# A transformer trunk in float32 on one core: four groups of seven products behind the last 256 columns, with a planner that counts work

## The chip, the cores and the metric

The kernel runs on one core of a Trainium2 chip. Its time is the device time of one execution in microseconds (us). A core has TensorE (PE in the profile, PEld is its weight load), VectorE (DVE), ScalarE (ACT), GpSimd (POOL) and SyncE (SP), each with an instruction queue of its own that it works off in order, and 16 DMA engines.

## What is computed

Two layers on 256 tokens of width 1024, all in float32, then a last RMSNorm. The change concerns the four channel mixers (two SwiGLUs in each layer, 2816 wide):

```python
def swiglu(h, w_gate, w_up, w_down):
    return (jax.nn.silu(h @ w_gate) * (h @ w_up)) @ w_down

for l in range(DEPTH):                     # DEPTH = 2, D_MODEL = 1024, SEQ = 256, D_FF = 2816
    x = x + 0.5 * swiglu(rms_norm(x, ffn1_norm[l]), ffn1_w_gate[l], ffn1_w_up[l], ffn1_w_down[l])
    ...                                    # two kinds of attention, x = x + concat(out_a, out_b) @ w_out[l]
    x = x + 0.5 * swiglu(rms_norm(x, ffn2_norm[l]), ffn2_w_gate[l], ffn2_w_up[l], ffn2_w_down[l])
return rms_norm(x, final_norm)
```

In the order of execution there are four of them, called FFN1 to FFN4 here; a mixer with attention stands between FFN1 and FFN2 and between FFN3 and FFN4.

## The kernel before

**Splits.** Every float32 operand is held as a high part (a cast to fp32r) and a low part (the remainder), and every product is three matmuls: high by high, low by high, high by low. For weights, ACT makes the high part (`CAST w<-raw`) and DVE the low part (`w<-raw,w`), in halves of 128x1024. A *split* is one such half. Weights come by DMA of SP into six tiles `raw`, 1 MB each; split halves lie in a pool of 28 tiles of 128 partitions x 1024 that they share with h and x.

**The FFN.** The 2816 columns are five groups of 512 and a rest of 256. Of each group, gate and up are computed (8 weight steps of 128 rows in `tokens`, for two blocks of 128 tokens), then `gate` (silu on ACT), `hidden` (the product with up, on DVE: `s<-ps,hr,tmp`), then `turn`: eight transposes of h on PE, a cast on ACT and a subtraction on DVE per half. The transposed h goes into the down matmuls (`down`), whose four accumulators `accs` stay open in PSUM over the whole FFN. The down matmuls of group g-1 are done inside group g, in two halves of the output columns, each with a weight step of its own.

**Seven products.** For groups 2, 3 and 4 (`SEVEN`) the gate and up product is seen as a 2x2 block product, two blocks of tokens by two halves of the contraction on one side and gate and up on the other, and done with seven block products in place of eight (`by_seven`). One block product (`prod`) is 12 matmuls of 128x512. It needs sums of blocks: of x (`make_sums`, four sums, each with a subtraction or addition on DVE, a cast on ACT and a subtraction on DVE, into tiles `q` and `v`), of weights, and of the products. The tiles of weights of a group are a and d (gate, first and second half of the contraction) and b and c (up). Sums of weights are made in place: c is added to b and b to a by *gathers*, which are DMAs of POOL that read the weights again and add them to the tile, and two more (c to a, d to a) by DVE (`raw<-raw,raw`). The products p2 to p7 are combined by DVE (`put`, `tmp<-ps,tmp`); g0 and g1 go through the silu, and `up` makes the two halves of h.

**The order of the work.** PE, ACT, DVE and POOL keep the order of the program (`Kept`), except in parts of the attention. The order of weight steps is a list `specs`; `ahead(n)` emits splits up to half n, sums of weights (`prep`) and DMAs as far ahead as tiles are free. `weights()` takes the next step and calls `ahead` with a look of `look[0]` halves, set by hand (8 in an FFN, 6 in the mixer). So the place of a split in DVE's and ACT's queues is fixed by the calls of `weights()`. After the groups, FFN and mixer are joined by `ffn_close`, which finishes the down matmuls (`group` for those of group 4, `tail` for those of the rest), adds them to the residual xk (`res.add`) and starts the next norm (`pair`, `squares`, `stats`; `stats` ends with a power on POOL that gives r). At the very end `close` and `finish` do so for the output.

**Order of an FFN before:** group 0 plain, group 1 plain (with the sums of x), groups 2 to 4 as seven products, the last 256 columns (`gu`), then the end. In FFN1 the constants of the attention are made at the end of `ffn` (`aside`).

Of the kernel before, what the change touches and what calls it, by code (L numbers as in the profile page):

```python
# [27 lines left out]
AHEAD = 10  # L28
N_RAW, N_S4 = 6, 28
IN_FFN, IN_MIX = 8, 6  # L30
SEVEN = (2, 3, 4)
# [3 lines left out]
def trunk(ctx: ExitStack, tc: tile.TileContext, x, n1, g1, u1, d1, nm, w_in, sink,  # L35
# [111 lines left out]
    def emit_dma(i):  # L147
        s = specs[i]
        raws[s.key] = raw = wp.tile([P, s.kn, s.n], F32, tag="raw", bufs=N_RAW, name=nm_("raw"))
        for dst, src in s.moves(raw):  # L150
            if i > 1:
                sp.dma_start(dst, src)
            else:
                for k in range(s.kn):
                    sp.dma_start(dst[:, k:k + 1], src[:, k:k + 1])
                    yield
        if s.behind is not None:
            s.behind()
# [52 lines left out]

    def ahead(n):

        n = min(n, 2 * len(specs) - 1)
        while True:
            if at["split"] <= n and at["prep"] > at["split"] // 2:
                for _ in emit_split(*divmod(at["split"], 2)):
                    pass
                at["split"] += 1
            elif at["prep"] <= min(n // 2 + 1, len(specs) - 1) and at["dma"] > at["prep"] and \  # L220
                    (specs[at["prep"]].prep is None or at["split"] >= 2 * at["prep"]):
                if specs[at["prep"]].prep is not None:
                    specs[at["prep"]].prep()
                at["prep"] += 1
            elif at["dma"] < min(at["use"] + AHEAD, len(specs)) and (specs[at["dma"]].moves is None or len(raws) < N_RAW):
                if specs[at["dma"]].moves is not None:
                    for _ in emit_dma(at["dma"]):
                        pass
                at["dma"] += 1
            else:  # L230
                break
# [11 lines left out]
    for l in range(DEPTH):  # L243
        def ffn_specs(wg, wu, wd):
            down = lambda g, h: plain(wd[l], h * 512, 512, 4 * g, 4)
            for k0 in (0, 4):
                specs.extend(plain(w[l], 0, 512, k0, 4) for w in (wg, wu))
            for g in range(1, NGRP):
                downs = [down(g - 1, h) for h in range(2)]
                if g in SEVEN:  # L250
                    specs.extend(seven(wg[l], wu[l], g * 512, downs))
                else:
                    specs.extend(plain(w[l], g * 512, 512, k0, 4) for w in (wg, wu) for k0 in (0, 4))
                    specs.extend(downs)
            for k0 in (0, 4):
                def gu_moves(t, k0=k0, ws=(wg[l], wu[l])):
                    return [(t[:, :, h * 256:h * 256 + 256], rows(w, FF - 256, 256, k0, 4)) for h, w in enumerate(ws)]
                specs.append(Step(4, 512, gu_moves))
            specs.append(down(NGRP - 1, 0))
            specs.append(plain(wd[l], 0, D, 4 * NGRP, 2))  # L260
            specs.append(down(NGRP - 1, 1))
# [17 lines left out]
        for k0 in (0, 2):  # L279
# [3 lines left out]
            specs.append(Step(2, D, o_moves))  # L283
        fine.update(range(mixed + 2, len(specs)))
# [5 lines left out]
    class Norm:  # L290


        def __init__(self, g0, sums=len(SEVEN) > 0):
            self.g0, self.xs, self.sums = g0, [], sums
            self.xg, self.turned = [], []
            self.ss = tmp("nss", 2, (P, 2, 4))
# [36 lines left out]
        def make_sums(self):  # L333
# [5 lines left out]
            def make(x, y, op):  # L339
# [4 lines left out]
                act.copy(sm[:, :, 0:P], v)  # L344
                dve.tensor_tensor(sm[:, :, P:S], v, f(sm[:, :, 0:P]), op=ALU.subtract)
# [3 lines left out]
            s1 = make(b1, t1, ALU.subtract)  # L349
            yield  # L350
            s2 = make(s1, t0, ALU.add)
            yield
            make(t1, t0, ALU.subtract)
            yield
            make(b0, s2, ALU.subtract)
# [12 lines left out]
        def stats(self, n=512):  # L368
# [7 lines left out]
            dve.tensor_scalar_mul(self.hr, self.r, 0.5)  # L376

# [189 lines left out]
    def ffn(norm, aside=None, before=None, final=False):  # L567
# [31 lines left out]
        def by_seven(h, g):  # L599

# [6 lines left out]

            m1, m7 = flat(), flat()
            act.copy(m1, prod(norm.quarter(0, 0), weights()))
            act.copy(m7, prod(norm.summed(2), weights(held=True)))  # L610
            hT = turn(h, 2)
            p2 = prod(norm.quarter(0, 1), weights())
            g0 = put(flat(), p2, m1, ALU.add)
            p3 = prod(norm.summed(3), weights())
            silu(g0, g0, 0)
            down(hT, g - 1, 0, weights())
            h = blk(F32)
            p5 = prod(norm.summed(0), weights())
            late = g == max(SEVEN)
            p6 = prod(norm.summed(1), weights(look[0] - 5 if late else 0, late))  # L620
            u2 = put(flat(), p6, m1, ALU.subtract)
            u3 = put(m7, m7, u2, ALU.add)
            p4 = prod(norm.quarter(1, 1), weights(look[0] - 4 if late else 0, late))
            g1 = put(m1, p4, u3, ALU.subtract)
            w = weights(look[0] - 3 if late else 0)
            silu(g1, g1, 1)
            put(u3, u3, p5, ALU.subtract)
            put(u2, u2, p5, ALU.subtract)
            put(u2, u2, p3, ALU.add)
            up(h, u2, g0, 0)  # L630
            up(h, u3, g1, 1)
            down(hT, g - 1, 1, w)
            return h

        def turn(hs, n):
            out_ = []
            for i in range(n):
# [11 lines left out]
        def down(hT, g, h, w):  # L649
            tokens(accs[h], [None] * (2 * g) + hT, w, 4 * g, last=(FC - 1, G4 - 1) if final and h else FC - 1)  # L650
# [14 lines left out]
        tokens(gs, norm.xs, weights(), 4)  # L665
        g = gate(gs)
        tokens(us, norm.xs, weights(), 4)
        h = hidden(g, us)
        for n in range(1, NGRP):
            sums = norm.make_sums() if n + 1 == min(SEVEN, default=0) else iter(())  # L670
            if n in SEVEN:
                look[0] = IN_FFN - max(0, n - 2) if before is not take_x else IN_MIX
                h = by_seven(h, n)
                continue
            gs = [bank(), bank()]
            tokens(gs, norm.xs, weights(), 0)
            hT = turn(h, 2)
            norm.copies()
            tokens(gs, norm.xs, weights(), 4)
            g = gate(gs)  # L680
            next(sums, None)
            us = [bank(), bank()]
            for k0 in (0, 4):
                tokens(us, norm.xs, weights(), k0)
                next(sums, None)
            h = hidden(g, us)
            for hh in range(2):
                down(hT, n - 1, hh, weights())
                if hh == 0:
                    next(sums, None)  # L690

        gu = [bank(), bank()]
        tokens(gu, norm.xs, weights(), 0)
        hT = turn(h, 2)
        tokens(gu, norm.xs, weights(), 4)
        h = hidden(gate([b[:, 0:256] for b in gu]), [b[:, 256:512] for b in gu])
        if aside is not None:
            aside()
        return accs, hT, lambda: turn(h, 1)

    BY_TOKENS = [(k, t) for t in range(2) for k in range(2)]
    G4 = 4 * (NGRP - 1)

    def ffn_end(parts, last):

        accs, hT, rest = parts
        hT = [None] * (2 * (NGRP - 1)) + hT
        hE = []
        look[0] = IN_MIX
        w = {0: weights()}  # L710

        def group(h, order, a=None, c=slice(None), first=0):
            tokens(a or accs[h], hT, w[h], G4, first=first, last=last[h], order=order, cols=c)

        def tail(h, order=BY_TOKENS, a=None, c=slice(None)):
            tokens(a or accs[h], [None] * (2 * NGRP) + hE, w["rest"], 4 * NGRP, last=last[h], order=order, cols=c, h=h)

        group(0, [(k, t) for k in range(3) for t in range(2)])
        hE.extend(rest())
        group(0, [(3, t) for t in range(2)])  # L720
        w["rest"] = weights()
        w[1] = weights(2)
        return group, tail

    def ffn_close(parts, nxt):
        group, tail = ffn_end(parts, (FC - 1, G4 + 3))
        res = Residual(nxt, parts[0])
        group(1, [(0, t) for t in range(2)])
        tail(0)
        for t in range(2):  # L730
            res.add(0, t)
        tail(1)
        ahead(2 * at["use"] - 2 + look[0])
        group(1, [(1, t) for t in range(2)])
# [3 lines left out]
        group(1, [(2, t) for t in range(2)])  # L738
        group(1, [(3, t) for t in range(2)])
# [239 lines left out]
    for l in range(DEPTH):  # L979
        final = l == DEPTH - 1  # L980
        parts = ffn(norm, attention_constants, take_x) if l == 0 else ffn(norm)
        norm_m = Norm(16 + l * 8, False)
        ffn_close(parts, norm_m)
        norm2 = Norm(32 + l * 8)
        mix(l, norm_m, norm2)
        parts = ffn(norm2, final_gain if final else None, final=final)
# [30 lines left out]
    accs = parts[0]  # L1017
    group, tail = ffn_end(parts, ((FC - 1), FC - 1))
    dve.tensor_tensor(xk[:, 1, 512:D], xk[:, 1, 512:D], accs[1][1], op=ALU.add)
    group(1, [(k, 0) for k in range(2)])  # L1020
    tail(0)
    for t in range(2):
        close(t, 0, 512, accs[0][t])
    group(1, [(k, 0) for k in (2, 3)])
    tail(1, [(k, 0) for k in range(2)])
    close(0, 512, 512, accs[1][0])
    finish(0)
    for c in (0, 256):
        acc = bank()[:, 0:256]
        cols = slice(c, c + 256)  # L1030
        group(1, [(k, 1) for k in range(4)], [None, acc], cols, G4)
        tail(1, [(k, 1) for k in range(2)], [None, acc], cols)
# [32 lines left out]
```

## Time and profile before

| | |
|---|---|
| time, median of 3 runs | 935.24 us (934.86 to 935.65) |
| the profiled execution | 935.0 us, of which the span 933.2 us |
| PE busy | 921.1 us, 99% of the span |
| DVE busy | 759.9 us, 81% |
| ACT busy | 566.8 us, 61% |
| POOL busy | 55.0 us, 6% |
| DMA | 194.58 MB, mean 208 GB/s |

Instruction rows give the place (a helper's line, L50, for nearly all), the engine, the operation, output and inputs by the program's names, partitions x elements, and a count. Timeline rows begin with the start and the length in us; an idle time before them and what ended it stand in brackets. Rows of groups end with busy us, the mean ns of one, and the idle time before them with what ended it. Matmuls are pipelined, so that a length of one in a row of groups is more than the distance between two; distances are taken from starts in the timeline.

### The profile page before, as it was taken

What the parts mean: (1) busy time and instruction counts of PE and PEld (TensorE: products, weight loads), DVE (VectorE), ACT (ScalarE), POOL (GpSimd) and SP (SyncE); (2) the same over time, 40 slices, a digit from 0 to 9 for tenths busy, and PEclk for the clock granted to TensorE, in tenths of its full rate; (3) what the DMA queues carried; (4) which work ended last, traced back from release to release, by engine and by line L of the source; (5) the groups of instructions that cost most, each with busy time, mean ns of one, the idle gap of its engine ahead of it and who ended that gap; (6) DMA issues with size and microseconds to landing.
All of it is one profiled execution on the core that took longest, in us unless ns stands there. A gap on an engine that the chain in (4) does not pass through costs nothing.

```text
span 933.2 us, 12665 instructions
## 1 busy us (share of the span) xinstructions
PE 921.1 (99%) x4796; PEld 780.7 (84%) x4796; DVE 759.9 (81%) x1074; ACT 566.8 (61%) x889; POOL 55.0 (6%) x73
## 2 busy tenths in 40 slices
PE   8999999999999999999999999999999999999997
PEld 6888878799898888888888888888999888888886
DVE  6759999869866588999776799996697566799994
ACT  7837576457745657576475466565577476466561
POOL 0400000000000001000000000000000000001011
PEclk9999999999999999999999999999999999999999
DMA  9996898827335858797767597887462367597831
GB/s 334 347 233 200 251 271 270 235 97 217 131 93 178 271 135 261 191 269 271 240 236 204 140 299 203 238 283 218 144 187 91 136 213 198 145 299 203 248 113 46
DMA packets 110893, 194.58 MB, mean 208 GB/s; under 512 B 3566, under 2 KB 31280, under 8 KB 110832
## 3 DMA queue, kind: packets, MB, share of 16 engines
q1 hardware_dynamic: 96528, 166.74, 52.8%
q0 software_dynamic: 12928, 25.46, 15.4%
q10 hardware_dynamic: 1376, 1.57, 0.5%
q8 instruction: 37, 0.61, 0.3%
q14 instruction: 24, 0.20, 0.1%
HBM read 192.71 MB, written 1.05 MB: 208 GB/s over the span
## 4 chain that ended last, share of the span: by engine, by line
PE 93%; DVE 4%; issue 1%; DMA 0%; ACT 0%; POOLq 0%; POOL 0%; ACTq 0%; DVEq 0%
PE ps L50 93%; DVE w L50 3%; DVE s L50 1%; DMA xk<-in_x_dram 0%; DVE tmp L50 0%; DVE raw L50 0%; ACT w L50 0%; DVE distA L50 0%; DVE xk L50 0%; DVE distB L50 0%; POOLq L1060 0%; POOL rf L50 0%; ACTq L50 0%; DVE lsum L50 0%; DVEq L50 0%
## 5 line engine op out<-in xcount | busy, mean ns | idle before, releaser
L50 PE MATMUL ps<-w,s 128*128 128x512 f32 (+1 forms) x2754 | 641.3, 391 | 1.2 <-DVE s L50 1.1
L50 PEld LDWEIGHTS ps<-w,s 128*128 128x128 f32 x2754 | 511.3, 188 | 107.5 <-DVE s L50 1.6
L50 DVE TENSOR_TENSOR w<-raw,w 128x1024 fp32r<-128x1024 f32 (+1 forms) x440 | 460.4, 1093 | 59.3 <-ACT w L50 58.1
L50 ACT CAST w<-raw 128x1024 fp32r<-128x1024 f32 (+1 forms) x440 | 391.1, 948 | 91.9 <-DVE raw L50 69.6
L50 PE MATMUL ps<-w,q 128*128 128x512 f32 x432 | 101.9, 389 | 0.0
L50 PEld LDWEIGHTS ps<-w,q 128*128 128x128 f32 x432 | 81.1, 188 | 16.8
L50 PE MATMUL ps<-s,w 128*128 128x256 f32 x672 | 84.0, 285 | 0.0
L50 PEld LDWEIGHTS ps<-s,w 128*128 128x128 f32 x672 | 81.7, 191 | 1.1
L50 ACT ACTIVATE s<-ps,gcol 128x256 fp32r<-128x256 f32 (+1 forms) x80 | 31.5, 488 | 47.0 <-PE ps L50 47.0
L50 DVE TENSOR_TENSOR raw<-raw,raw 128x1024 f32<-128x1024 f32 x48 | 56.5, 1219 | 0.0
L50 ACT CAST s<-ps 128x512 fp32r<-128x512 f32 x48 | 26.1, 593 | 46.5 <-PE ps L50 46.5
L50 POOL DMA_DIRECT2D raw<-in_ffn_w_up_dram x24 | 31.1, 1296 | 352.9 <-DVE w L50 166.5
L50 DVE TENSOR_TENSOR s<-ps,s 128x512 fp32r<-128x512 f32 x48 | 31.0, 684 | 25.1 <-ACT s L50 25.1
L50 PE MATMUL ps<-ident,s 128*128 128x128 f32 x304 | 39.9, 274 | 0.6 <-DVE s L50 0.6
L50 PEld LDWEIGHTS ps<-ident,s 128*128 128x128 f32 x304 | 35.0, 141 | 5.9 <-DVE s L50 1.4
L50 ACT ACTIVATE tmp<-tmp,r 128x512 f32<-128x512 f32 x24 | 17.3, 722 | 34.0 <-DVE tmp L50 34.0
L50 ACT ACTIVATE s<-s,negm 128x256 f32<-128x256 f32 x64 | 31.9, 500 | 6.3 <-DVE negm L50 6.1
L50 PE MATMUL ps<-w,v 128*128 128x512 f32 x144 | 34.6, 389 | 0.0
L50 ACT CAST q<-tmp 128x512 fp32r<-128x512 f32 x20 | 12.4, 621 | 35.3 <-DVE tmp L50 35.2
L50 PEld LDWEIGHTS ps<-w,v 128*128 128x128 f32 x144 | 27.0, 188 | 5.6
L50 DVE SCALAR_TENSOR_TENSOR s<-ps,gcol,s 128x256 fp32r<-128x256 f32 x48 | 20.3, 478 | 12.5 <-ACT s L50 12.4
L50 ACT COPY tmp<-ps 128x512 f32<-128x512 f32 x24 | 14.0, 584 | 22.6 <-PE ps L50 22.5
(106 smaller groups left out, 427.0 us busy)
## 6 DMA issues: line engine op xcount, KB each, us to landing
raw<-in_ffn_w_down_dram SPq DMA_DIRECT2D x44, 1024.0 KB, 5.4
raw<-in_ffn_w_gate_dram SPq DMA_DIRECT2D x39, 1024.0 KB, 6.0
raw<-in_ffn_w_up_dram SPq DMA_DIRECT2D x39, 1024.0 KB, 5.4
raw<-in_ffn_w_up_dram POOLq DMA_DIRECT2D x24, 1024.0 KB, 10.5
raw<-in_w_in_dram SPq DMA_DIRECT2D x14, 1024.0 KB, 5.1
raw<-in_ffn_w_gate_dram SPq DMA_DIRECT2D x8, 512.0 KB, 6.4
raw<-in_ffn_w_up_dram SPq DMA_DIRECT2D x8, 512.0 KB, 7.3
raw<-in_w_in_dram SPq DMA_DIRECT2D x8, 512.0 KB, 6.3
```

What stands on the lines that cost most here:

```text
L50: ins = issue(*a, **k)
```

## The change

- `SEVEN` is gone: in every FFN group 0 is plain, the last 256 columns come right behind it, and groups 1 to 4 are all seven products. The sums of x are made during the last columns. The order of the seven products is the same; the sums are made in another order.
- `ffn` returns the accumulators, the transposed h of the last columns (made in group 1) and a function that turns the h of group 4. `ffn_close` (and the end of the kernel) does the tails first, then the transposes of group 4's h, then the down matmuls of group 4. The attention constants move from `ffn` to `ffn_close`, behind these transposes.
- `ahead` is replaced by a planner in parts: `act_once` emits one step, `fill(until)` emits splits until a count of DVE's work reaches a count of PE's work, `chain` calls `fill` before an operation that waits for PE, and `take` takes the next step and emits only the splits that it still needs. The counts start anew after the first part of each FFN's group 0.
- The DMAs of weights have an order of their own (`order`: b, a, d, c, then the down weights).
- Gathers are put in a list and issued only after the norm's `stats` (`held`, `flush`).
- Copies of the first two products (`act.copy(m, acc)`) stand behind the casts that `fill` puts ahead of them.

```diff
-            s.behind()
+            behind.append(s.behind)
+            if not held[0]:
+                flush()
...
+    def act_once(n):
+        i, j = divmod(at["split"], 2)
+        if at["split"] <= n and at["prep"] > i:
+            for _ in emit_split(i, j):
+                pass
+            clk["dve"] = max(clk["dve"], freed.get(at["split"] - LIVE, 0.0)) + SPLIT
+            ready[at["split"]] = clk["dve"]
+            at["split"] += 1
+            return True
...
+    def fill(until):
+        while clk["dve"] < until and at["split"] < min(2 * at["use"] + LIVE, 2 * len(specs)) and act_once(at["split"]):
+            pass
+        while load_once():
+            pass
...
+    def chain(cost, release=None):
+        r = clk["pe"] if release is None else release
+        fill(r)
+        clk["dve"] = max(clk["dve"], r) + cost
+
+    def take():
+        i = at["use"]
+        at["use"] += 1
+        ahead(2 * i + 1)
...
...
+            for g in range(1, NGRP):
+                specs.extend(seven(wg[l], wu[l], g * 512, [down(g - 1, h) for h in range(2)]))
             specs.append(plain(wd[l], 0, D, 4 * NGRP, 2))
-            specs.append(down(NGRP - 1, 1))
+            specs.extend(down(NGRP - 1, h) for h in range(2))
...
         dve.tensor_scalar_mul(self.hr, self.r, 0.5)
+            held[0] = False
+            flush()
...
-            act.copy(m1, prod(norm.quarter(0, 0), weights()))
-            act.copy(m7, prod(norm.summed(2), weights(held=True)))
-            hT = turn(h, 2)
+            for m, xo in ((m1, norm.quarter(0, 0)), (m7, norm.summed(0))):
+                acc = product(xo)
+                fill(clk["pe"])
+                act.copy(m, acc)
...
-            p4 = prod(norm.quarter(1, 1), weights(look[0] - 4 if late else 0, late))
+            p4 = product(norm.quarter(1, 1))
+            chain(0.65)
             g1 = put(m1, p4, u3, ALU.subtract)
-            w = weights(look[0] - 3 if late else 0)
             silu(g1, g1, 1)
+            chain(2.7)
             put(u3, u3, p5, ALU.subtract)
             put(u2, u2, p5, ALU.subtract)
             put(u2, u2, p3, ALU.add)
             up(h, u2, g0, 0)
+            chain(0.7)
             up(h, u3, g1, 1)
-            down(hT, g - 1, 1, w)
-            return h
+            clk["up"] = clk["dve"]
+            down_(1)
+            return hs, h
...
+        part(gs, 4)
+        fill(clk["pe"])
         g = gate(gs)
+        part(us, 4)
+        chain(1.4)
         h = hidden(g, us)
+        norm.copies()
+        sums = norm.make_sums()
         gu = [bank(), bank()]
+        part(gu, 0)
+        for _ in range(2):
+            fill(clk["dve"] + 1.0)
+            sum_step()
+        clk["pe"] = max(clk["pe"], clk["up"]) + 0.9
+        chain(1.3, clk["pe"] + 0.6)
         hT = turn(h, 2)
+        for _ in range(2):
+            sum_step()
+        part(gu, 4)
+        chain(0.9)
         h = hidden(gate([b[:, 0:256] for b in gu]), [b[:, 256:512] for b in gu])
+        hE, h = by_seven(hT, h, 1)
+        for n in range(2, NGRP):
+            h = by_seven(None, h, n)[1]
+        held[0] = True
+        look[0] = IN_MIX
+        return accs, hE, lambda: turn(h, 2)
...
+        we = weights(3, True)
+        for h in range(2):
+            tail(accs[h], hE, we, h)
+        hT = turn_()
         if aside is not None:
             aside()
+        group(accs[0], hT, weights(), ALL)
         for t in range(2):
             res.add(0, t)
-        tail(1)
-        ahead(2 * at["use"] - 2 + look[0])
-        group(1, [(1, t) for t in range(2)])
+        w = weights()
+        group(accs[1], hT, w, ALL[:4])
         for j in range(2):
             nxt.pair(j)
         res.squares(0)
-        group(1, [(2, t) for t in range(2)])
-        group(1, [(3, t) for t in range(2)])
+        group(accs[1], hT, w, ALL[4:])
         for t in range(2):
             res.add(1, t)
```

At the end of the kernel the same order holds: both tails, the transposes, group 4's down matmuls for the first half of the columns, then those of the second half, the second block of tokens in two pieces of 256 columns; the tails there are 6 matmuls of 512 columns where they were 12 of 256.

## The prediction

> **What bounds the kernel now.** I read the page first (busy shares, then the chain that ended last), then the chain in order of time, then windows over three successive seven groups in the first FFN and in the third.
>
> ```profile
> span 933.2 us, 12665 instructions
> PE 921.1 (99%) x4796; PEld 780.7 (84%) x4796; DVE 759.9 (81%) x1074; ACT 566.8 (61%) x889; POOL 55.0 (6%) x73
> ...
> PE 93%; DVE 4%; issue 1%; DMA 0%; ACT 0%; POOLq 0%; POOL 0%; ACTq 0%; DVEq 0%
> ...
> 9.12 122.98 PE ps L50 x554
> ...
> 179.75 742.84 PE ps L50 x3983
> ...
> 69.80:186.50 116.70, 114.94 (x519) 93.66 (x518) 113.41 (x127) 73.96 (x88) 5.13 (x4) 1.00 0.83 245
> 531.30:644.30 113.00, 113.00 (x518) 93.80 (x517) 105.80 (x112) 68.76 (x81) 5.18 (x4) 1.00 0.84 245
> ```
>
> TensorE is the bound: from 179.75 to 922.59 the chain is one piece of it. Only between 132 and 180 us does DVE stand in the chain. The windows (length; busy PE, PEld, DVE, ACT, POOL; granted clock; DMA share; GB/s) show the same work twice, groups 2 to 4 and the last columns: 116.70 in the first FFN, 113.00 in the third, so DVE's late splits there cost 3.7. DVE has little room in either (113.41 of 116.70, 105.80 of 113.00).
>
> **A, matmuls.** A product of a seven group is 12 matmuls 128x512, and seven of them replace eight, so the fourth group saves 12 in each of four FFNs: 48. The end of the kernel turns 12 matmuls of 256 columns into 6 of 512, so 42 fewer are left.
>
> ```profile
> 370.30 11.04 PE L50 MATMUL ps<-w,s 128*128 128x512 f32 x48
> 381.18 2.89 PE L50 MATMUL ps<-w,q 128*128 128x512 f32 x12
> ```
>
> The next piece starts 10.88 after 48 matmuls began: 0.2267 each, 2.72 for a product. 42 x 0.2267 = **-9.5**. The 12 narrow ones I count at nothing: behind them DVE's last closes, in a queue of their own, end later than TensorE (low end -1.4). **B**: the 3.7 of the first FFN went with its former order, -3.7 (low end -3.7, high end 0, if they come back in groups 2 to 4). Together -13.2.
>
> **DVE's load.** A fourth seven group adds six splits and four additions of raw tiles per FFN and the sums of partial products.
>
> ```profile
> L50 DVE TENSOR_TENSOR w<-raw,w 128x1024 fp32r<-128x1024 f32 x336 | 394.0, 1220 | 52.6 <-ACT w L50 51.5
> L50 DVE TENSOR_TENSOR raw<-raw,raw 128x1024 f32<-128x1024 f32 x48 | 56.5, 1219 | 0.0
> 364.46 9.16 DVE L50 TENSOR_TENSOR w<-raw,w 128x1024 fp32r<-128x1024 f32 x8
> ```
>
> 24 splits and 16 additions, at the pitch of eight in a row (9.16/8 = 1.145), are 46, and 28 operations on tmp at about 0.7 are 20: DVE goes from 760 to some 826 of 933. That is no wait by itself, but it decides who is late when something is queued badly. The steps below come from the new order of each engine's instructions, laid beside the old durations.
>
> **C, end of the fourth group.** The second half of the down weights used to be split ahead of the last product's sums. Now, in group 4 of every FFN, that split stands on DVE behind g1, three puts and two ups, which wait for product p4. TensorE has only the first half of the down matmuls to do after p4: 12 x 0.2267 = 2.72.
>
> ```profile
> 377.14 0.68 DVE L50 TENSOR_TENSOR tmp<-ps,tmp 128x512 f32<-128x512 f32 x1
> 377.75 1.22 DVE L50 TENSOR_TENSOR w<-raw,w 128x1024 fp32r<-128x1024 f32 x1
> 378.88 2.00 DVE L50 TENSOR_TENSOR tmp<-tmp,ps 128x512 f32<-128x512 f32 x3
> 380.92 1.42 DVE L50 SCALAR_TENSOR_TENSOR s<-tmp,hr,tmp 128x512 f32<-128x512 f32 x2
> ```
>
> From g1 to the last up is 382.34 - 377.14 = 5.2, with one split inside; without it 4.1. Then the split, 1.22, and 0.1 of hand-over: 5.4. TensorE waits 5.4 - 2.72 = 2.7 (2.4 if the hand-overs overlap, 3.6 if another split comes between). Four times: **+10.8** (9.6 to 14.4).
>
> **D, transposes of the last h.** Both tails now stand before them, and group 4's down matmuls, which read the transposed h, directly behind. Before, matmuls of other columns lay between.
>
> ```profile
> 319.53 1.04 PE L50 MATMUL ps<-ident,s 128*128 128x128 f32 x8
> 320.32 3.01 PE L50 MATMUL ps<-w,s 128*128 128x512 f32 x12
> 320.17 1.08 ACT L50 CAST s<-ps 128x512 fp32r<-128x512 f32 x2 [5.62 <-PE ps L50]
> 320.78 1.29 DVE L50 TENSOR_TENSOR s<-ps,s 128x512 fp32r<-128x512 f32 x2 [3.10 <-ACT s L50]
> ```
>
> TensorE is free at 320.32; the first half's low part is ready after the first of two subtractions, 320.78 + 0.65 = 321.43, while one matmul can go on the cast alone: about 0.95 of wait (0.7 to 1.2). Four times: **+3.8**.
>
> **E, the residual's adds.** The adds of the first half stand on DVE behind six look-ahead splits, and only 12 matmuls follow before the next norm's transposes need them; in the first FFN the attention constants stand in front too.
>
> ```profile
> 172.77 0.18 DVE L50 COPY gcol<-ps 128x34 f32<-128x34 f32 x1
> ...
> 176.18 0.15 DVE L50 TENSOR_SCALAR gsub<-gcol 128x1 f32<-128x1 f32 x1
> 182.57 0.69 DVE L50 TENSOR_TENSOR xk<-xk,ps 128x512 f32<-128x512 f32 x1 [0.67 <-PE ps L50]
> ```
>
> From the end of the transposes TensorE has 0.95 + 36 x 0.2267 = 9.1 of work and wait. DVE has 1.75 (subtractions), 6 x 1.145 = 6.9 and 2 x 0.69: 10.0, of which I take 0.7 late (the splits may wait less than listed). With the constants (176.33 - 172.77 = 3.6, and a table for the exponential on ACT) 5.0. FFN1 5.0, FFN2 and FFN3 0.7 each: **+6.4** (2 to 8).
>
> **F, the first gather.** c of group 1 is added to b by a DMA of POOL, held until the norm's pow. On ACT the cast of b's first half stands ahead of the gate's silu, so the silu, h and the transposes of h wait for that DMA to land. The transposes keep their places on TensorE, at 36.29 and 497.76, because part of the last columns fills the room that group 1's first products had.
>
> ```profile
> 27.49 0.72 POOL L50 TENSOR_TENSOR r<-ms,mhalf 128x2 f32<-128x2 f32 x1 [25.98 <-DVE ms L50]
> 43.64 1.38 POOL L50 DMA_DIRECT2D raw<-in_ffn_w_up_dram  x1 [3.16 <-ACT tmp L50]
> 28.36 1.28 ACT L50 ACT_TABLE_LOAD   x1
> 29.65 1.27 ACT L50 ACTIVATE tmp<-ps,r 128x512 f32<-128x512 f32 x2
> 58.13 2.00 ACT L50 CAST w<-raw 128x1024 fp32r<-128x1024 f32 x2 [8.01 <-DMA raw<-in_ffn_w_up_dram]
> 36.29 0.93 PE L50 MATMUL ps<-ident,s 128*128 128x128 f32 x7
> 34.16 1.41 DVE L50 SCALAR_TENSOR_TENSOR s<-ps,hr,tmp 128x512 f32<-128x512 f32 x2
> DMA to landing us min/median/max: 8.3/10.5/15.6
> 483.57 0.72 POOL L50 TENSOR_TENSOR r<-ms,mhalf 128x2 f32<-128x2 f32 x1 [77.98 <-DVE ms L50]
> 497.76 0.49 PE L50 MATMUL ps<-ident,s 128*128 128x128 f32 x3
> 24.00:28.00 4.00, 4.00 (x19) 3.30 (x19) 3.14 (x5) 3.89 (x6) 0.51 (x1) 1.00 1.05 387
> ```
>
> If the gather takes x from issue to landing, it is there at 28.2 + x. Then follow: the cast 1.0, the table 1.28, both silus 1.27, two more casts 1.9, the last one's split 1.22, the two operations of h 1.41, hand-overs 0.1: 8.2. So h is ready at 36.4 + x, and TensorE waits about x + 0.2. For x the near rows are 8.3, 10.5 and 15.6, and 14.5 for the first gather of before (58.13 - 43.64), whose surroundings are the nearest: transfers at full rate, as at 24 to 28 us (387 GB/s). I take 12.5, between the median and that one: **+12.7** (8.5 to 15.8). The Trainium skill (DMA: Bandwidth & Descriptors, SWDGE vs HWDGE vs iDMA) says that the two kinds of queue feed different internal queues and each engine goes round-robin between them; by that the gather would not stand behind the queued loads, x would be nearer the median, and the sum 2 lower. The 14.5 above speaks against it, without excluding it.
>
> In the third FFN the same order gives h at 484.3 + x + 6.9 (no table), needed at 497.76: x - 6.6. There I take the median 10.5: **+4.0** (1.7 to 9.0). The second and fourth FFN follow a mixer, where b is fetched long before: nothing.
>
> **G, what follows from F.** After such a wait the four sums of x alternate between DVE and ACT.
>
> ```profile
> 44.89 0.62 ACT L50 CAST q<-tmp 128x512 fp32r<-128x512 f32 x1 [0.92 <-DVE tmp L50]
> ```
>
> Four times (0.69 + 0.62 + 0.69) = 8.0, two splits 2.3, h's casts and subtractions 2.4, the last columns' silus and ups 1.8: 14.5. TensorE has 0.8 of transposes and 24 + 24 matmuls, 10.9: 11.7. So 2.8 more in FFN1 and in FFN3, and about 1 each for splits late in groups 2 and 3 (0 to 2.2): **+7.6** (0 to 10).
>
> **Sum.** -13.2 + 10.8 + 3.8 + 6.4 + 12.7 + 4.0 + 7.6 = +32.1. The profiled execution took 935.0 (span 933.2 and 1.8 around it), the median of the runs is 935.24: **967**. All low ends give 945; all high ends give 987, B lost included, but the three waits that depend on a transfer are not likely to be at their worst together.
>
> **Rivals.** *The waits are covered* (faster): TensorE's matmuls count in full, and DVE and ACT catch up within the order, since nothing but TensorE bounds 93% of the chain. Price: 935.0 - 13.2 = 922. It decides once C to G together stay below 11; against it, C and D alone, which hang on no transfer, give 14.6. Chance 0.05. *Only C and D remain*, because gathers land at once: 936.4, no change; x would have to be below 3 where 8.3 is the least seen. Chance 0.02. *DVE bound over four groups* (slower still): a seven group needs 18 splits and 4 additions (22 x 1.145 = 25.2), 0.7 + 2.0 + 1.4 + 1.3 + 1.4 of sums, ups and transposes: 32.0, where TensorE needs 30.8; four in a row use up the lead, 1.2 for each group and FFN in the worst case, 4 x 4 x 1.2 = 19: 975 to 986. For it speaks 113.41 of 116.70; against, 105.80 of 113.00 in the third FFN. Chance 0.15. *A lower clock after long waits*: if TensorE comes out of F's and G's waits slowed, one product at half speed after each of three costs 3 x 2.72 = 8: 975. Every window here has a clock of 1.00 and no wait as long. Chance 0.08. The Trainium skill (TensorE: Matmul & The Clock Gate, Part 1: The HAM clock gate) has the clock halved after an idle window of about 3.4 us, until about 3.4 us of activity; by that it would be 1.7 for each, an estimate, and 5 in all. No row of before shows it.
>
> **How the numbers follow.** The forecast's own case has 0.70 and holds 945 to 980; the DVE bound and the clock add to the top, the covered waits lie below, so that 944 to 984 leaves out no more than two in ten. No change is what lies within 0.2%, 1.9 us, about what a measurement of this kernel can tell: 0.02. Faster has 0.06 with errors in the sum, slower 0.92.
>
> **What would show it.** In the changed profile: ACT's cast of w at about 28 idle before it until a gather, TensorE idle 8 to 16 behind 36 and 2 to 9 in the third FFN; four waits of 2 to 3 on a DVE split at the ends of the fourth groups; about 1 behind the transposes of each last h; some 5 before the first mixer. The matmuls 128x512 fewer by 42, at a pitch of 0.227. The forecast is wrong if the first gather lands in under 6, or if the chain stays TensorE's throughout.

## The result: 1009.26 us, 7.9% slower than before

The changed kernel takes 1009.26 us (median of 4 runs, 1007.82 to 1013.52), the kernel before 935.44 in the same runs: a ratio of 1.079 (95% interval 1.078 to 1.081). The direction was forecast, the size was not: 967 was predicted, 984 was the upper end. Of the +75.6 in the span (933.2 to 1008.8) the forecast's terms explain less than half.

The page of the changed kernel:

```profile
span 1008.8 us, 12747 instructions
PE 937.4 (93%) x4742; PEld 776.3 (77%) x4742; DVE 826.5 (82%) x1142; ACT 593.6 (59%) x921; POOL 63.0 (6%) x81
...
PE 38%; DVE 36%; issue 10%; ACT 10%; DMA 4%; SPq 1%; POOL 0%; ACTq 0%; POOLq 0%; DVEq 0%
```

DVE's work came out as counted (826 expected, 826.5). But the chain is no longer TensorE's: it goes back and forth between TensorE (38%), DVE (36%) and ACT (10%). Windows over the four FFNs, each up to the second transposes of the next norm, or to the end, first of the kernel before and then of the changed one (length; busy PE, PEld, DVE, ACT, POOL; granted clock; DMA share; GB/s):

```profile
0.00:192.97 192.97, 187.19 (x851) 153.11 (x851) 162.03 (x195) 123.84 (x171) 18.34 (x43) 1.00 0.86 263
296.87:475.11 178.24, 178.24 (x818) 148.11 (x817) 149.29 (x163) 110.14 (x142) 8.45 (x7) 1.00 0.76 228
475.11:650.75 175.64, 175.64 (x818) 146.48 (x816) 147.66 (x164) 107.07 (x142) 8.50 (x7) 1.00 0.78 230
754.63:933.20 178.57, 172.25 (x803) 143.70 (x801) 144.47 (x167) 100.03 (x127) 15.05 (x12) 0.99 0.63 186
```

```profile
0.00:225.61 225.61, 193.41 (x838) 154.10 (x839) 180.41 (x214) 130.79 (x179) 19.70 (x45) 0.95 0.80 235
329.36:518.67 189.31, 179.78 (x805) 144.95 (x804) 165.36 (x180) 116.64 (x150) 9.77 (x8) 1.00 0.75 220
518.67:714.83 196.16, 183.28 (x805) 147.57 (x804) 163.96 (x181) 113.73 (x150) 10.98 (x9) 0.97 0.75 217
818.70:1008.80 190.10, 173.29 (x785) 140.28 (x783) 161.50 (x184) 106.75 (x135) 15.05 (x13) 0.99 0.61 177
```

The FFNs take 32.6, 11.1, 20.5 and 11.5 more; the mixers between them take the same. DVE has 16 to 18 more to do in each. Where TensorE waits, in its timeline (the wait and what ended it in brackets):

```profile
45.44 7.99 PE L49 MATMUL ps<-w,s 128*128 128x512 f32 x24 [14.25 <-ACT tmp L49]
...
217.01 0.33 PE L49 MATMUL ps<-ident,xk 128*128 128x128 f32 x1 [3.72 <-DVE xk L49]
...
490.90 8.01 PE L49 MATMUL ps<-w,s 128*128 128x512 f32 x34 [2.18 <-DVE w L49]
...
539.56 8.33 PE L49 MATMUL ps<-w,s 128*128 128x512 f32 x24 [3.52 <-ACT tmp L49]
```

These are F (14.25 and 3.52), E (3.72) and C (2.18) of the prediction, each near its term. The rest is in many waits of 0.3 to 1.6 inside the groups. Windows from one pair of transposes of h to the next, for groups 1 to 4 of FFN2 and then group 4 of FFN3 (the last two with the tails):

```profile
363.80:394.20 30.40, 30.40 (x137) 25.19 (x136) 28.42 (x30) 18.97 (x23) 2.57 (x2) 1.00 0.73 219
394.20:426.80 32.60, 31.49 (x142) 25.52 (x141) 32.42 (x34) 21.18 (x25) 2.59 (x2) 1.00 0.88 247
426.80:461.50 34.70, 31.87 (x141) 25.27 (x140) 31.94 (x33) 19.17 (x22) 1.29 (x1) 1.00 0.75 220
461.50:498.70 37.20, 32.40 (x141) 25.10 (x140) 31.61 (x33) 18.57 (x21) 0.00 (x0) 1.00 0.71 227
658.30:697.20 38.90, 35.12 (x141) 27.58 (x140) 31.66 (x33) 18.59 (x21) 0.00 (x0) 0.91 0.75 230
```

Without a wait TensorE's matmuls and transposes take 30.4 (group 1) to 30.8. Group 3 has 34.7 in every FFN, group 4 37.2 to 38.9. In group 3 DVE is busy for 31.9 of that and idle for 2.8: late and idle at once. The three seven groups of FFN2 in the kernel before:

```profile
353.10:383.90 30.80, 30.80 (x141) 25.61 (x140) 29.57 (x32) 20.05 (x23) 2.57 (x2) 1.00 0.88 246
383.90:414.70 30.80, 30.80 (x141) 25.60 (x140) 30.32 (x32) 20.04 (x23) 2.57 (x2) 1.00 0.87 241
414.70:445.60 30.90, 30.90 (x142) 25.63 (x141) 30.80 (x33) 19.57 (x22) 0.00 (x0) 1.00 0.72 239
```

TensorE does not wait in them, but DVE is busy for 29.6, 30.3 and 30.8: in the third group it had no room left before the change.

Put together, in us: matmuls saved and FFN1's former waits -14.6 (4 x 2.72 + 3.7); F with the slow matmuls behind it +23.4 (17.0 and 6.4, the delays of the first transposes of h); the four groups in four FFNs +54.5 (about 9 in groups 2, 16 in groups 3, 29 in groups 4); the ends of the FFNs +11.9. That is +75.2 of 75.6.

### The profile page after: what moved, and what is told of

Read it like the earlier page. It is cut to its first block, busy times and chain, and to the rows that moved or that the text cites. A ratio compares the mean times of both kernels' runs of the same rounds, so it can differ in the third digit from the quotient of the medians.

```text
span 1008.8 us, 12747 instructions
## 1 busy us (share of the span) xinstructions
PE 937.4 (93%) x4742; PEld 776.3 (77%) x4742; DVE 826.5 (82%) x1142; ACT 593.6 (59%) x921; POOL 63.0 (6%) x81
## 4 chain that ended last, share of the span: by engine, by line
PE 38%; DVE 36%; issue 10%; ACT 10%; DMA 4%; SPq 1%; POOL 0%; ACTq 0%; POOLq 0%; DVEq 0%
PE ps L49 38%; DVE w L49 20%; DVE tmp L49 7%; ACT w L49 6%; DVE raw L49 5%; DMA raw<-in_ffn_w_up_dram 3%; DVE s L49 3%; ACT tmp L49 1%; ACT s L49 1%; DMA xk<-in_x_dram 1%; DVE q L49 1%; DVE xk L49 1%; SPq L151 1%; ACT q L49 0%; ACT L49 0%
## 5 line engine op out<-in xcount | busy, mean ns | idle before, releaser
L49 PE MATMUL ps<-w,s 128*128 128x512 f32 x2508 | 609.3, 399 | 50.8 <-DVE w L49 20.2
L49 PEld LDWEIGHTS ps<-w,s 128*128 128x128 f32 x2508 | 471.2, 192 | 166.2 <-DVE w L49 31.6
L49 DVE TENSOR_TENSOR w<-raw,w 128x1024 fp32r<-128x1024 f32 (+1 forms) x464 | 488.6, 1102 | 81.0 <-ACT w L49 79.5
L49 ACT CAST w<-raw 128x1024 fp32r<-128x1024 f32 (+1 forms) x464 | 415.5, 953 | 95.4 <-DVE raw L49 64.7
L49 PE MATMUL ps<-w,q 128*128 128x512 f32 x576 | 137.6, 391 | 4.3 <-DVE w L49 4.3
L49 PEld LDWEIGHTS ps<-w,q 128*128 128x128 f32 x576 | 107.6, 188 | 29.1 <-DVE w L49 7.1
L49 DVE TENSOR_TENSOR raw<-raw,raw 128x1024 f32<-128x1024 f32 x64 | 75.3, 1219 | 0.0
L49 PE MATMUL ps<-w,v 128*128 128x512 f32 x192 | 46.7, 393 | 0.2
L49 PEld LDWEIGHTS ps<-w,v 128*128 128x128 f32 x192 | 35.6, 188 | 9.0 <-ACT tmp L49 1.1
L49 ACT ACTIVATE s<-s,negm 128x256 f32<-128x256 f32 x64 | 31.9, 501 | 6.6 <-DVE negm L49 6.3
L49 DVE TENSOR_TENSOR tmp<-ps,tmp 128x512 f32<-128x512 f32 x48 | 32.9, 685 | 0.0
L49 DVE TENSOR_TENSOR tmp<-tmp,ps 128x512 f32<-128x512 f32 x48 | 31.5, 685 | 1.1
```

The source lines that it names most:

```text
L49: ins = issue(*a, **k)
```

## Why DVE idles while it is late

In group 3 of FFN2 of the changed kernel, DVE's rows and then ACT's:

```profile
433.36 0.69 DVE L49 TENSOR_TENSOR tmp<-ps,tmp 128x512 f32<-128x512 f32 x1
435.78 2.36 DVE L49 TENSOR_TENSOR w<-raw,w 128x1024 fp32r<-128x1024 f32 x2 [1.73 <-ACT w L49]
...
434.08 0.72 ACT L49 ACTIVATE tmp<-tmp,r 128x512 f32<-128x512 f32 x1 [3.67 <-DVE tmp L49]
434.71 1.99 ACT L49 CAST w<-raw 128x1024 fp32r<-128x1024 f32 x2
```

DVE makes g0 (433.36). ACT has waited 3.67 us for it with the silu at the head of its queue. DVE's next split needs a cast that stands behind that silu: 0.63 and 1.04 later. So DVE stands for 1.73. In the kernel before, at the same place:

```profile
392.60 0.68 DVE L50 TENSOR_TENSOR tmp<-ps,tmp 128x512 f32<-128x512 f32 x1
393.20 1.21 DVE L50 TENSOR_TENSOR w<-raw,w 128x1024 fp32r<-128x1024 f32 x1
...
395.59 1.05 ACT L50 CAST w<-raw 128x1024 fp32r<-128x1024 f32 x1 [3.03 <-DVE raw L50]
396.54 0.72 ACT L50 ACTIVATE tmp<-tmp,r 128x512 f32<-128x512 f32 x1
```

The silu stands behind the casts there, and DVE goes on without a wait. The change had swapped two lines, which its list above does not name: `silu(g0, g0, 0)` now comes ahead of the step of p3. The wait of 1.7 to 1.8 behind g0 stands in groups 1, 3 and 4 of every FFN. Group 1, with a lead in splits, still takes 30.4; in group 2 of FFN2 the next cast was done in time and there is no wait.

The theory after the result: a group lasts as long as DVE's own work (about 32) plus DVE's waits for ACT, once the lead in splits is gone. Rivals: only the order of the queues; only DVE's work; transfers or free tiles; and, apart from the groups, the clock.

## Experiments

Ratios are to the kernel before, with their 95% intervals.

**e1_cap**: no split of b ahead of the first silu in FFN1 and FFN3.

```diff
-        if at["split"] <= n and at["prep"] > i:
+        if at["split"] <= min(n, cap[0]) and at["prep"] > i:
...
+        if b1_late:
+            cap[0] = 2 * (at["use"] + 5) - 1
         part(gs, 4)
...
         h = hidden(g, us)
+        cap[0] = 10 ** 9
```

> Only the splits of b of group 1 are kept behind the gate and the product with up in the first and third FFN; the rest is the changed kernel. Theory 'gather ahead of the silu': TensorE's idle of 14.25 at 31 us and of 3.5 at 536 us goes, and with it the slow matmuls right behind (24 in 7.8 us where 5.44 is usual), some -14 to -23 in all: 986 to 995. Rival 'DVE's work decides': the delay comes back in the groups behind, because DVE has the same work to do: over 1003.

1003.52 us (1.073, 1.071 to 1.075): 6 gained, outside the theory's range and at the edge of the rival's (over 1003). TensorE's timeline:

```profile
41.43 1.04 PE L49 MATMUL ps<-ident,s 128*128 128x128 f32 x8
...
61.41 1.29 PE L49 MATMUL ps<-ident,s 128*128 128x128 f32 x4 [8.02 <-DVE s L49]
```

The first transposes come 11.8 earlier (53.27 before), but 8.0 of it is lost again 20 us later: the same splits now stand ahead of the sums of x. There each sum (DVE, ACT, DVE) has a cast put between, and DVE waits 1.64 for it, three times.

**e2_look2**: every step emits two halves more.

```diff
-        ahead(2 * i + 1)
+        ahead(2 * i + 1 + 2)
```

> Every step emits the splits of one step more than it needs (2 halves further ahead); no work is added or taken. Theory 'order of the queues': groups 3 and 4, which take 34.7 and 37 to 39 us where TensorE's matmuls need 30.8, are late because a split is queued only when it is needed, behind operations that wait for TensorE; with two halves in hand group 3 comes to 32 to 33 and the waits of 2.2 behind group 4 go: -15 to -30 in all, 980 to 994. Rival 'DVE's work': DVE is busy 32 of each 34.7, order can give little: 1004 to 1010.

1000.42 us (1.070, 1.068 to 1.071), between the two. The 9 gained lie in the groups 4, where the wait of 2.2 (C) is gone: they take 35.6 in every FFN, 1.6 less in FFN2 and FFN4 and 3.2 less in FFN1 and FFN3, where slow matmuls stood behind that wait. Group 3 does not move:

```profile
422.52:457.28 34.76, 31.92 (x142) 25.29 (x140) 32.00 (x33) 19.16 (x22) 1.29 (x1) 1.00 0.75 221
```

The same 1.73 of DVE idle behind g0 is there. Earlier emission alone doesn't change which operation stands ahead of which around the silu, so the order theory failed in this form for group 3.

**e3_close**: the residual's adds ahead of the look-ahead, the constants later.

```diff
-        group(accs[0], hT, weights(), ALL)
+        group(accs[0], hT, weights(5, True), ALL)
...
         res.squares(0)
+        if aside is not None:
+            more_constants()
```

> At the end of the FFN the adds to the residual stand ahead of the look-ahead splits, and the attention constants (but for the gains) behind the norm's first transposes. Theory: the wait of 3.7 + 0.3 before the first mixer goes, and 0.3 to 0.9 in each other FFN: -4 to -6. Rival: the splits, now later, make the next stage late by as much: within 2.

1018.84 us (1.089, 1.088 to 1.091): 10 slower than the changed kernel, worse than the rival. The adds came early, and the splits behind them were late for the second down weights. This wait stands at the end of the first three FFNs (TensorE, then DVE, end of FFN2):

```profile
513.00 2.57 PE L49 MATMUL ps<-w,s 128*128 128x512 f32 x10 [1.46 <-DVE w L49]
...
511.73 8.03 DVE L49 TENSOR_TENSOR w<-raw,w 128x1024 fp32r<-128x1024 f32 x7
```

In FFN1 a wait of 3.4 for the residual stands one pair of transposes later. These waits are part of the 10; the rest was not taken apart.

**e4_fixed**: the planner undone, a fixed look-ahead.

```diff
     def fill(until):
+        return
...
-        ahead(2 * i + 1)
+        ahead(2 * i + look[0])
...
         for n in range(2, NGRP):
+            look[0] = {1: 8, 2: 8, 3: 7, 4: 6}[n]
```

> The planner alone is undone: each step emits splits a fixed 8 halves ahead (7 in group 3, 6 in group 4), as before the change, and the counts decide nothing; four groups, the order of groups and the gathers stay. Theory 'order of the queues': groups 2 to 4 fall to 31 to 32.5 each: -30 to -45, 964 to 979. Rival 'DVE's work, four groups in a row': group 4 and perhaps 3 stay above 33.5 since a group needs 32 of DVE and the lead is used up: 985 to 1005.

990.16 us (1.058, 1.057 to 1.060), in the range of the rival. Groups 2 and 3 of FFN2:

```profile
385.58:419.86 34.28, 32.42 (x142) 25.29 (x141) 32.36 (x34) 20.77 (x25) 2.59 (x2) 1.00 0.87 246
419.86:453.28 33.42, 31.83 (x142) 25.34 (x141) 31.55 (x34) 20.11 (x24) 1.29 (x1) 1.00 0.87 247
```

Group 3 is DVE's 31.55 plus one wait of 1.73 behind g0, and little else. Without the planner 19 of the 74 are gained: it is a part, not the main cause.

**e5_silu**: the silu behind the casts that follow.

```diff
             g0 = put(flat(), p2, m1, ALU.add)
-            silu(g0, g0, 0)
...
             p5 = product(norm.summed(1))
+            silu(g0, g0, 0)
```

> The changed kernel with one operation of ACT moved: the silu of g0 stands behind the casts of the two splits that follow it, in every seven group. Theory 'DVE waits for ACT behind the silu': DVE adds g0, then idles 1.73 us for a silu (0.63) and a cast (1.05); where DVE is the bound that is 1.7 of each group. Groups 3 fall from 34.7 to 33.0, groups 4 by 1.7, groups 2 of the first and third FFN by 1.7: -15 to -20, 989 to 994. Rival 'the idle is only slack that TensorE's waits make': it comes back elsewhere, over 1004.

999.97 us (1.069, 1.067 to 1.070). Group 3 of FFN2 loses 1.8, as expected:

```profile
421.15:454.05 32.90, 31.34 (x141) 25.45 (x140) 31.91 (x33) 19.17 (x22) 1.29 (x1) 1.00 0.80 233
```

But only 9 of the 15 to 20 arrived, between the two ranges. Groups 2 of FFN1 and FFN3 hardly moved (33.8 to 33.3, 33.7 to 33.9). Group 4 of FFN2 got 0.3, that of FFN4 got longer (37.3 to 38.4): the 34 matmuls behind the last wait of FFN2 took 9.3 to the next piece where the changed kernel's took 7.8. That is the clock, below.

**e6_noadd**: the additions of raw tiles left out.

```diff
-                for h in (0, 2):
-                    x_, t_ = [raws[i][:, h:h + 2] for i in (x, to)]
-                    dve.tensor_tensor(t_, t_, x_, op=ALU.add)
+                for i in (x, to):
+                    raws[i]
```

> The changed kernel without the additions of raw weight tiles on DVE (four of 1.15 us in each seven group; so two of the seven products are formed from other sums), everything else in its order. Theory 'DVE's work and idle make the length of a group': 34.7 falls by 4.6 to TensorE's 30.8 in group 3, and groups 2 and 4 fall to 30.8 plus the wait behind the last product: -30 to -45, 964 to 979. Rival 'DMA or slots': a group waits for transfers or for tiles to come free, then groups stay over 33: over 995.

985.99 us (1.054, 1.052 to 1.056). Groups 2 and 3 of FFN2, with 4.6 less for DVE and all else in its order:

```profile
387.47:418.31 30.84, 30.84 (x142) 25.60 (x140) 26.74 (x29) 19.57 (x23) 2.62 (x2) 1.00 0.87 242
418.31:449.12 30.81, 30.81 (x141) 25.60 (x140) 25.70 (x28) 18.76 (x22) 1.29 (x1) 1.00 0.72 228
```

They are at TensorE's length. So no transfer and no tile holds up groups 2 and 3. Group 4 stays at 37.3 there, although DVE has 4.6 less to do: the wait behind g0 (1.6 on TensorE), C (2.2) and slow matmuls remain. This is why the gain is 23 and not 30.

**e7_bsilu**: the kernel before with the swap of the silu alone.

```diff
-            p3 = prod(norm.summed(3), weights())
             silu(g0, g0, 0)
+            p3 = prod(norm.summed(3), weights())
```

> The kernel before the change with the same single swap that the change made in its seven groups: the silu of g0 ahead of the splits that come with p3. Theory 'DVE waits for ACT behind the silu': DVE, which was busy 30.3 to 30.8 of 30.8 in the later groups, loses up to 1.7 in each of 12 groups: +8 to +20, 943 to 955. Rival 'without the fourth group there is slack': within 2 of the kernel before.

950.39 us (1.016, 1.014 to 1.017): **+15 for two lines in another order**. Group 3 of FFN2 goes from 30.8 to 32.6, group 4 from 30.8 to 32.4; group 2 keeps its 30.8:

```profile
389.76:422.39 32.63, 31.49 (x142) 25.35 (x140) 30.79 (x33) 19.86 (x23) 2.57 (x2) 1.00 0.83 229
```

**e8_best**: e4 with the silu behind p3's step, a and b late in FFN1 and FFN3 (e1's cap, from a on), and a look-ahead in the tails.

```diff
-            silu(g0, g0, 0)
             p3 = product(norm.summed(3))
+            silu(g0, g0, 0)
...
+            cap[0] = 2 * (at["use"] + 4) - 1
...
-        we = weights(3, True)
+        we = weights(0, True)
```

> Four groups of seven, with a fixed look-ahead of 8, 8, 7, 6 halves, the silu of g0 behind p3's splits, no split of group 1 ahead of the silu of group 0 in the first and third FFN, and the look-ahead of the tails filled. From the run with the fixed look-ahead alone (990): 12 to 14 groups less 1.7 each, and 8 to 12 at the first transposes: 955 to 965. If DVE's 32 per group against TensorE's 30.8 were hidden by the lead too, 935 or less; theory 'DVE's work' says it can't be wholly: over 945.

964.86 us (1.031, 1.029 to 1.032), as expected from the sum of the parts. The look-ahead in the tails moved a wait: TensorE no longer waits before the first mixer, but 2.3 behind the last h of each of the first three FFNs.

**e9_order**: e5, with the next step's splits ahead of the copies of products.

```diff
                 acc = product(xo)
+                ahead(2 * at["use"] + 1)
                 fill(clk["pe"])
                 act.copy(m, acc)
```

> The changed kernel with ACT's order mended twice in every seven group: the silu of g0 behind the casts of the splits that follow, and each copy of a product (m1, m7) behind the casts that the next product needs. Theory 'a group lasts as long as DVE's work plus its waits for ACT': with the silu alone group 3 of the second FFN took 32.9, of which 1.2 were waits behind the copies; so 31.7 to 32.0 here, and the time 5 to 9 less than with the silu alone (1000): 991 to 995. What then stays over TensorE's 30.8 is DVE's own work. Rival 'the copies' place costs nothing': 999 to 1001.

1000.1 us (1.068, 1.065 to 1.070), the same as e5. The edit moved nothing on ACT, since the splits it asked for had been emitted; the casts behind the copies belong to a later step. The copies' place remains untested.

**e10_warm**: matmuls whose result is not used in the two waits for the gather.

```diff
+        for _ in range(spare):
+            pe.matmul(accs[1][1], lhsT=norm.xs[0][:, 0, 0:P], rhs=norm.xs[0][:, 0], start=True, stop=True)
         gu = [bank(), bank()]
```

> The changed kernel with matmuls that compute nothing that is used, put on TensorE in the waits for the first gather: 54 in the first FFN, 15 in the third. Theory 'the clock falls in a long wait': the 24 matmuls behind, 7.8 and 8.2 us in the changed kernel, come back to 5.4 each, and the first transposes of h stand 2.4 and 2.7 earlier; in all -2 to -5. Rival 'the matmuls behind the wait are slow for another reason' (operands that come late): no change in them, and the time the same or longer by what the extra matmuls overrun.

1020.86 us (1.091, 1.089 to 1.092). The filler waited for the silu too, so it lengthened the path instead of filling the gap. Still it tells the clock's part. TensorE's timeline:

```profile
44.94 15.33 PE L49 MATMUL ps<-s 128*128 128x512 f32 x54 [13.95 <-ACT tmp L49]
60.10 5.61 PE L49 MATMUL ps<-w,s 128*128 128x512 f32 x24
```

The 54 take 15.2 to the next piece, 2.9 more than 54 x 0.2267, and the 24 that were slow in the changed kernel take 5.4 again. In FFN3 the 15 take 5.7, 2.3 more than usual, and the 24 behind them 5.4. Slow are the first matmuls behind the wait, whichever they are. The changed kernel's windows before, in and behind that wait have a granted clock of 1.00, 0.57 and 0.69:

```profile
14.60:31.20 16.60, 16.59 (x75) 13.44 (x73) 12.09 (x20) 12.71 (x24) 3.12 (x5) 1.00 1.07 373
31.20:45.44 14.24, 0.00 (x0) 0.00 (x0) 3.28 (x3) 3.67 (x5) 5.28 (x24) 0.57 1.08 291
45.44:53.27 7.83, 7.83 (x24) 6.20 (x25) 5.47 (x6) 6.27 (x12) 4.03 (x6) 0.69 0.57 169
```

24 matmuls took 7.83 where 5.44 is usual: 2.4, and 2.7 in FFN3. The Trainium skill (TensorE: Matmul & The Clock Gate, Part 1: The HAM clock gate) states that the clock halves after an idle window of about 3.4 us and returns after a busy one of about the same length. The trace agrees that the clock is low behind these waits and then returns; the price is larger, 2.3 to 2.9 per wait where the forecast's estimate from that page was 1.7.

**e11_sums**: e8 without the tails' look-ahead, and b's splits also behind the sums of x (the cap is lifted in two steps).

```diff
         h = hidden(g, us)
-        cap[0] = 10 ** 9
+        if b1_late:
+            cap[0] = 2 * first + 1
...
         for _ in range(2):
             sum_step()
+        cap[0] = 10 ** 9
         part(gu, 4)
```

> As the run with four mends (fixed look-ahead, silu behind p3's splits, no split of group 1 ahead of the first silu; 965), but without look-ahead in the tails, and in the first and third FFN the splits of b of group 1 also stand behind the sums of x. Theory 'what stands in a queue behind the gather is late': TensorE's waits of 2.6 and 7.6 at 48 to 59 us go, and the wait of 2.3 behind each last h: 10 to 18 less, 947 to 955. Rival 'DVE's work comes back later': over 958.

959.92 us (1.026, 1.024 to 1.028): 5 gained, in the range of the rival. The waits named went down from 7.6 to 2.6 and from 2.3 to 0.2, but group 1 of FFN1 now takes 36.6 (32.9 in e8), and a wait of 2.6 before the first mixer is back: most of the lateness came back later.

**e12_pool**: e11 with the additions on POOL.

```diff
-                    dve.tensor_tensor(t_, t_, x_, op=ALU.add)
+                    pool.tensor_tensor(t_, t_, x_, op=ALU.add)
```

> As the run before it in this call, with the additions of raw weight tiles done by POOL in place of DVE. Theory 'DVE's work': DVE is relieved of 4.6 in each seven group, comes to 27.4 of TensorE's 30.8, and groups 2 to 4 take 30.8: 930 to 940, less than the kernel before if nothing else turns up. Rival 'POOL is too slow or in DVE's way': an addition there takes over twice as long and what reads it waits: over 955.

1030.16 us (1.099, 1.097 to 1.102). One addition takes 2.9 us on POOL, 1.2 on DVE, and ACT's casts waited 178 us for them in all:

```profile
L49 POOL TENSOR_TENSOR raw<-raw,raw 128x1024 f32<-128x1024 f32 x64 | 184.7, 2897 | 244.4 <-DVE w L49 244.4
```

**e13_lead**: e11 with a longer look-ahead.

```diff
-            look[0] = {1: 8, 2: 8, 3: 7, 4: 6}[n]
+            look[0] = {1: 8, 2: 9, 3: 9, 4: 8}[n]
```

> As the run with four mends (960: fixed look-ahead of 8, 8, 7, 6 halves, silu of g0 behind p3's splits, splits of b late in the first and third FFN), with a look-ahead of 8, 9, 9, 8 halves. Theory 'a group is as long as DVE's own work': groups 2 to 4 still take 31.5 to 32.5 each, since DVE is busy 31.3 to 32.3 in them, and the time stays within 4 of 960. Rival 'the lead hides it': DVE's 0.9 per group over TensorE's 30.8 comes out of splits made earlier, groups 2 and 3 come to 30.9: 945 to 953.

961.48 us (1.028, 1.027 to 1.030), within 4 of e11, as expected. Windows over the four groups of FFN2 with the tails, e11 and then e13:

```profile
345.14:471.96 126.82, 124.92 (x558) 101.50 (x556) 125.18 (x130) 78.94 (x92) 6.45 (x5) 1.00 0.81 241
```

```profile
341.90:470.21 128.31, 124.18 (x558) 101.76 (x557) 127.04 (x132) 81.18 (x94) 6.45 (x5) 1.00 0.83 246
```

DVE is busy 125.2 of 126.8 and 127.0 of 128.3. With the queues in order DVE itself is full. More lead only moves the waits: groups 2 to 4 of FFN2 take 34.8, 32.2 and 30.9 where e11 has 31.8, 31.7 and 32.8, so one by one they are not the 31.5 to 32.5 that were expected.

**e14_blook, e14b_bsilu2**: the kernel before with the full look-ahead in FFN1 too; and with the silu one step later still.

```diff
-                look[0] = IN_FFN - max(0, n - 2) if before is not take_x else IN_MIX
+                look[0] = IN_FFN - max(0, n - 2)
```

```diff
             p3 = prod(norm.summed(3), weights())
+            w = weights()
             silu(g0, g0, 0)
-            down(hT, g - 1, 0, weights())
+            down(hT, g - 1, 0, w)
```

> The kernel before the change with the look-ahead of the other FFNs (8, 8, 7, 6 halves) in the first FFN too, where it is 6. Theory 'the lead decides in the first FFN, where DVE was late by 3.7': 2 to 4 less, 931.5 to 933.5, and less than either kernel. Rival 'DVE has no time for a lead there': within 1 of the kernel before.

> The kernel before the change with the silu of g0 one step later still, behind the splits that come with the down weights. Theory 'only a silu ahead of casts that DVE needs next costs': behind p3's splits it already stands behind two of them, so nothing is gained: within 1.5 of the kernel before. Rival 'every step later gains': 1.5 to 4 less, in the first FFN.

937.80 us (1.002, 1.001 to 1.003) and 937.36 us (1.002, 1.001 to 1.003). The first is 2.0 slower than the kernel before, the second 1.6, both just outside the rival's and the theory's bounds of 1 and 1.5. Neither gains; the kernel before stays the fastest of all.

## Why the prediction was wrong, point by point

- **A: right.** The pitch stayed at 0.227 us where nothing waits, and the groups that don't wait take 30.4 to 30.8. **B: right**: FFN1's former waits went, and its four groups take 137.9 where those of FFN3, which had no such waits before, take 137.7.
- **C: right in mechanism, a little small in size**: 2.2 for each, where 2.7 was forecast and 2.4 was the low end. In FFN2 the five splits start at 489.62, behind the ups, and TensorE goes on at 490.90.
- **D, E: the waits named were right** (0.2 to 0.8 behind each last h against 0.95; 3.7 before the first mixer against 5.0), the ends of the FFNs as a whole 11.9 against 10.2. Putting the adds ahead was no cure: it cost 10 more (e3).
- **F: right in mechanism and near in size.** The first gather was issued at 28.78 and read at 42.35, 13.6 later against 12.5; in FFN3 it was read 10.1 after its issue against 10.5:

```profile
28.78 1.47 POOL L49 DMA_DIRECT2D raw<-in_ffn_w_up_dram  x1
...
42.35 1.04 ACT L49 CAST w<-raw 128x1024 fp32r<-128x1024 f32 x1 [10.54 <-DMA raw<-in_ffn_w_up_dram]
```

  With the clock, which the forecast left to a rival of chance 0.08, F cost 23.4 and not 16.7. One thing was missed: TensorE stopped before the last columns and not only before the transposes, since the matmuls of the last columns too were released by the silu (that they take over the bank it reads is inferred, not shown).
- **G, and the step "That is no wait by itself" before C: here the forecast failed.** For FFN1 and FFN3 it had 2.8 each for the sums, which did not come (hE's transposes stand 11.8 behind h's, without a wait), and 1 each for splits late in groups 2 and 3, which came (group 2 takes 33.8 and 33.7 there, 32.5 in FFN2 and FFN4); for FFN2 and FFN4 it had nothing. Measured: 13.6 a FFN in the groups, 54.5 in all, of which C is 8.7. Two things were missing. DVE's 32.0 against TensorE's 30.8 was there as a rival, with chance 0.15 and 19 at most, and belonged in the sum: e11 and e13 show DVE full over four groups. Against that rival the forecast held an average, 105.80 of 113.00, which has the last columns in it; by groups DVE was already at 30.3 and 30.8 of 30.8 in the kernel before. And DVE's idle behind g0, 1.73 in groups 3 and 4, appears in no term: the two swapped lines are in the whole diff (not in the part shown above), but were not weighed. e7 prices that swap at 15 in the kernel before, and e5 gives 1.8 for each group 3. A third part is the planner's order: without it 19 of the 74 go (e4), some of them in the groups. These prices overlap and can't be added up.
- **The rival 'lower clock' was real**: behind F's two waits it cost 2.4 and 2.7, and besides F the clock fell to 0.96 and 0.91 in the fourth groups of FFN1 and FFN3, where no wait is over 2.2 us. The 34 matmuls behind C's wait of 2.2 take either 7.8 to 7.9 or 9.3 to 9.5 to the next piece: the longer time in two of four FFNs here, in all four of e6 and e9, in one of e10. The forecast had no term for it.
- **The rival 'waits covered'** was wrong: with ACT's order mended (e11, e13) four seven groups still fill DVE.

What stays open: the place of the copies (e9 did not move them), how much of the 54.5 is the planner's alone, and how short a wait lowers the clock.

## What to carry to other kernels

Where two engines feed each other, an operation of the first that waits for the second must not stand ahead of what the second needs next: one such place in a loop costs a full hand-over wherever the second has no lead left (1.7 us here, 15 over the kernel in e7, while group 2 of its FFN2, which had a lead, paid nothing). Trading matmuls for sums pays only as long as the engine that makes the sums has room in that very stage: DVE, 82% busy over the span, was 92% busy in group 3 here, and 99% over FFN2's groups once the queues were in order. A gain on TensorE that is bought with work on a full engine is paid back at that engine's rate.

## What was not expected of the hardware

After a wait of 14 us TensorE's next 24 matmuls took 7.8 us in place of 5.4, and in windows with no wait over 2.2 the clock fell to 0.91 and 0.96 in two FFNs and stayed at 1.00 in two others with the same waits. An addition of 128x1024 float32 took 2.9 us on POOL and 1.2 on DVE.
